# Memory and x read by feature as well: transposes of both left out, k-tiles of memory and weights in turns, memory's scale moved to the split of the values

## The chip, the cores and the metric

The kernel runs on one core of a Trainium2 chip, in one launch. The metric is the device time of one execution in microseconds, the median of several runs. Five engines matter: TensorE (PE; its weight loads are shown apart as PEld), VectorE (DVE), ScalarE (ACT), GpSimd (POOL), and SyncE (SP), which here issues nearly all DMAs. Each engine works through its own queue in order, and waits on semaphores of the others.

## The reference, cut to what matters

One layer of a streaming encoder in float32: 256 tokens, width 2048, 256 memory tokens.

```python
def reference(x, mem, positions, norm_mix_g, w_in, ...):
    h = rms_norm(x, norm_mix_g)
    x = x + hybrid_mixer(h, positions, w_in, conv_w, ...)
    h = rms_norm(x, norm_x_g)
    mem_n = rms_norm(mem, norm_mem_g)
    x = x + cross_attention(h, mem_n, w_xq, w_xkv, w_xo)
    h = rms_norm(x, norm_ffn_g)
    x = x + jnp.square(jax.nn.relu(h @ w_ff1)) @ w_ff2
    return rms_norm(x, norm_final_g)

def rms_norm(x, g):
    y = x * lax.rsqrt(jnp.mean(x * x, axis=-1, keepdims=True) + 1e-6)
    return y * g
...
    k, v = jnp.split(mem_n @ w_kv, 2, axis=-1)      # in cross_attention
```

`rms_norm` has two factors: a gain per feature and a scale per token. A product over the features needs the gain inside, but the token's scale can be multiplied in afterwards, at the rows of the product.

## The kernel before, in words

All large products run as three TensorE products of a cheaper number format (float32r): an operand is split into a rounded part (`whi`, `qh`) and the rest (`wlo`, `ql`), and hi x hi, hi x lo and lo x hi are added up in PSUM. The split of weights is `fetch` (L89): one DMA on SP brings a *quarter* of the features, 4 k-tiles of 128 rows by 512 columns, 1 MiB, into `raw` (3 buffers); ScalarE rounds it in two halves (L108), VectorE subtracts (L111); `whi` and `wlo` have 3 buffers of a half each. SP also issues the loads of all other tensors, in one fixed order.

`chunk` (L137) makes 512 output columns for 256 tokens: for each of the 4 quarters, 4 k-tiles, 2 halves of the tokens and three products (L151, L152, L153) of 512 columns. `blocks` (L177) is the form with weights as the stationary operand (L193, L194).

A *quad* holds 4 k-tiles of activations by feature (feature on the partitions, 256 tokens along the row), hi and lo. Activations come as rows of tokens, so they are transposed on TensorE against `ident`.

The order around the change, at the start of the program:

- `load_gains(0, ...)` (L242): memory's gains arrive as 16 rows and are transposed by TensorE (L248).
- `values(0)` (L334): the first 512 columns of the cross-attention's values. Its `chunk` calls `load_mem(c)` (L325) for each quarter: a load of memory's rows (L312), eight transposes (L262), then on ScalarE rounding with the gain (L275) and on VectorE the rest (L276). The first quarter's weights come in two DMAs (`rush`). The chunk's evacuation multiplies by the token scale of memory (L343), so it first takes the row squares of memory (L291) and `rms_cols`.
- gains of the other norms (L349, 48 rows, one transpose); four loads of x's rows (L352), their squares, `rms_cols`, and `scale_row` (L299), which spreads the scale of the tokens over the partitions as `rrow` by TensorE (L303).
- x by feature: 32 transposes (L364); ScalarE copies them out as `xt` (L367), which SP writes to a scratch `xt_d` in DRAM for the later residual (L368, read in `load_x`, L953); VectorE makes `xn` = x times gain times `rrow` (L371), and a split fills `h1` (L374, L375).
- `values(1)`; the four conv weights come as rows and are transposed by two TensorE instructions (L386); constants, positions, sine and cosine; `values(2)`, `narrow` (L204), `values(3)`; decay tables (L521), and the keys by `blocks` (L545), scaled by `mrow`, memory's scale spread over the partitions.

Then the mixer, the cross-attention (L963 on: keys and values are read back from DRAM and split, L970 and L971) and the MLP follow. The instructions of every engine are put in order ahead of the launch by a scheduler that goes by priorities (`high_priority`) and by its own estimate of when operands are there.

Of the kernel before, what the change touches and what calls it, by code (L numbers as in the profile page):

```python
# [17 lines left out]
P = 128  # L18
# [29 lines left out]
MAGIC = 1.5 * 2.0**23  # L48


@with_exitstack
def trunk(ctx: ExitStack, tc: tile.TileContext, x, mem, positions, norm_mix_g, w_in, conv_w, gdn_a_log, gdn_dt_bias,
          ret_gn_g, gdn_norm_g, w_out, norm_x_g, norm_mem_g, w_xq, w_xkv, w_xo, norm_ffn_g, w_ff1, w_ff2,
          norm_final_g, inv_freq, out):
# [21 lines left out]
    rushed = []  # L76

# [11 lines left out]
    def fetch(pieces, k, n, rush=False, hold=None, at=(0, 0)):  # L89


        raw = wp.tile([P, k * n], F32, name="raw", tag="raw", bufs=3)
        rv = raw.rearrange("p (k n) -> p k n", k=k)
        with tc.high_priority(offset=100000):
            for off, ap in pieces:
                src = ap.rearrange("(k p) n -> p k n", p=P)
                for ks in ((slice(0, k // 2), slice(k // 2, k)) if rush else (slice(0, k),)):
                    fetched.append(nc.sync.dma_start(rv[:, ks, off:off + ap.shape[1]], src[:, ks, :]).ins)
            got = []
            for i in range(2):  # L100
                if hold:
                    both = hold().both
                    hi, lo = (both[:, a:a + 2, :].rearrange("p a s -> p (a s)") for a in (0, 2))
                else:
                    hi, lo = (wp.tile([P, k * n // 2 + room], F32R, name=nm, tag=nm, bufs=3)[:, a:a + k * n // 2]
                              for nm, a, room in zip(("whi", "wlo"), at, (64, 0)))
                src = raw[:, i * k * n // 2:(i + 1) * k * n // 2]
                rounding = act.activation(hi, src, AF.Copy)  # L108
                if rush and not i:
                    rushed.append(rounding.ins)  # L110
                vec.tensor_sub(lo, src, hi.bitcast(F32))  # L111
                got.append((hi.rearrange("p (k n) -> p k n", n=n), lo.rearrange("p (k n) -> p k n", n=n)))
        return got
# [23 lines left out]
    def chunk(quads, pieces_of, evac, before=None, hold=None):  # L137

# [87 lines left out]
    vec.memset(warm, 0.0)  # L226
    act.activation(warm, warm, AF.Exp)
    ident = cp.tile([P, P], F32, name="ident")
    ones = cp.tile([P, P], F32, name="ones")
    vec.memset(ones, 1.0)  # L230
# [9 lines left out]
    gains = cp.tile([P, 64], F32, name="gains")  # L240

    def load_gains(c0, vectors):  # L242
        rows = sm.tile([48, P], F32, name="grow", tag="junk", bufs=1)
        n = 16 * len(vectors)
        for i, g in enumerate(vectors):
            nc.sync.dma_start(rows[16 * i:16 * (i + 1), :], g.rearrange("o (k p) -> (o k) p", p=P))
        gps = bank()
        pe.transpose(gps[:, :n], rows[:n], ident[:n, :n])  # L248
        vec.tensor_copy(gains[:, c0:c0 + n], gps[:, :n])

    with tc.high_priority(offset=200000):
        load_gains(0, (norm_mem_g,))
    G_MEM, G_MIX, G_X, G_FFN = 0, 16, 32, 48

    def to_feature(src, gain, quad):

        for f2 in range(2):
# [8 lines left out]
            qh, ql = quad  # L266
            if gain is None:
                h, l = qh[:, f2 * 2:f2 * 2 + 2, :], ql[:, f2 * 2:f2 * 2 + 2, :]
                act.activation(h, pv, AF.Copy)
                vec.tensor_sub(l, pv, h.bitcast(F32))  # L270
            else:
                for f in range(2):
                    k = f2 * 2 + f
                    g = gains[:, gain + k:gain + k + 1]
                    last = act.activation(qh[:, k, :], pv[:, f, :], AF.Copy, scale=g)  # L275
                    vec.scalar_tensor_tensor(ql[:, k, :], pv[:, f, :], g, qh[:, k, :].bitcast(F32),  # L276
                                             op0=ALU.mult, op1=ALU.subtract)
        return None if gain is None else last.ins
# [28 lines left out]
    def load_rows(c, src, rush, pieces=1):  # L307
        xc = kv.tile([P, NT, 512], F32, name="xc", tag="xc", bufs=8)
        rows = src[0, :, c * 512:(c + 1) * 512].rearrange("(t p) d -> p t d", p=P)
        with tc.high_priority(offset=rush):  # L310
            for ts in (slice(i * NT // pieces, (i + 1) * NT // pieces) for i in range(pieces)):
                nc.sync.dma_start(xc[:, ts, :], rows[:, ts, :])  # L312
# [12 lines left out]
    def load_mem(c):  # L325
        with tc.high_priority(offset=50000):
            xc = load_rows(c, mem, 50000 if c else 100000, 1 if c else 2)
            with tc.high_priority(offset=100000), nullcontext() if c else tc.issue_after(rushed[0]):
                ins = to_feature(lambda t, f: xc[:, t, f * P:(f + 1) * P], G_MEM + 4 * c, memq[c])
        mem_rows.append((xc, ins))  # L330

    mem_scale, mem_rows = [], []

    def values(n):  # L334
        vo = kv.tile([P, NT, 512], F32, name="vo", tag="vo", bufs=2)

        def evac_kv(t, ps, c0, c1):
            if not mem_scale:
                for c in range(4):
                    with tc.issue_after(mem_rows[c][1]):  # L340
                        row_squares(mem_rows[c][0], ssqm, c)
                mem_scale.append(rms_cols("nm", ssqm))
# [6 lines left out]
    load_gains(16, (norm_mix_g, norm_x_g, norm_ffn_g))  # L349
    h1 = [quad_a() for _ in range(4)]  # L350
    ssq1 = cp.tile([P, NT, 4], F32, name="ssq1")
    xcs = [load_rows(c, x, 0) for c in range(4)]  # L352
    for c in range(4):
        row_squares(xcs[c], ssq1, c)
    rstd1 = rms_cols("n1", ssq1)
    rrow = scale_row("rrow", rstd1)
    xt_d = dram.tile([P, KT, S], F32, name="xt_d", tag="xt_d", bufs=1)
    for k2 in range(8):
        ps = bank()
        pv = ps.rearrange("p (f s) -> p f s", f=2)  # L360
        for f in range(2):
            for t in range(NT):
                col = (2 * k2 + f) % 4 * P
                pe.transpose(pv[:, f, t * P:(t + 1) * P], xcs[k2 // 2][:, t, col:col + P], ident)  # L364
        xt = kv.tile([P, 2, S], F32, name="xt", tag="xt", bufs=2)
        xn = kv.tile([P, 2, S], F32, name="xn", tag="xn", bufs=2)
        act.activation(xt, pv, AF.Copy)  # L367
        nc.sync.dma_start(xt_d[:, 2 * k2:2 * k2 + 2, :], xt)  # L368
        for f in range(2):
            k = 2 * k2 + f  # L370
            vec.scalar_tensor_tensor(xn[:, f, :], pv[:, f, :], gains[:, G_MIX + k:G_MIX + k + 1], rrow,  # L371
                                     op0=ALU.mult, op1=ALU.mult)
        qh, ql = (a[:, k2 % 2 * 2:k2 % 2 * 2 + 2, :] for a in h1[k2 // 2])
        act.activation(qh, xn, AF.Copy)  # L374
        vec.tensor_sub(ql, xn, qh.bitcast(F32))  # L375

    values(1)

    cw_rows = kv.tile([96, 2, P], F32, name="cw_rows", bufs=1)
    for a in range(2):  # L380
        for j in range(2):
            nc.sync.dma_start(cw_rows[48 * j:48 * (j + 1), a, :], conv_w[0, 2 * a + j].rearrange("(b p) -> b p", p=P))
    cw = mc.tile([P, 4, 48], F32, name="cw")
    for a in range(2):
        ps = bank()
        pe.transpose(ps[:, :96], cw_rows[:, a, :], ident[:96, :96])  # L386
        vec.tensor_copy(cw[:, 2 * a:2 * a + 2, :], ps[:, :96].rearrange("p (j b) -> p j b", j=2))
# [142 lines left out]
    values(2)  # L530
    narrow(h1, w_in[0], C_GA, 32, decay_rows)
# [4 lines left out]
    rstdm = mem_scale[0]  # L536
# [303 lines left out]
    def gates():  # L840
# [23 lines left out]
        def of_delta_rule(j, yr, yg, quad, before=None):  # L864
            chunk(h1, cols(w_in[0], C_GZ + 512 * j), silu_gate(yg))
            chunk(h1, cols(w_in[0], C_TB + 512 * j), sig_gate(yg, yr), before=before)
            to_feature(lambda t, f: yg[:, t, f * P:(f + 1) * P], None, quad)
# [96 lines left out]
    for h in range(XH):  # L964
# [6 lines left out]
        split(vv, vr)  # L971
# [60 lines left out]
    for fb in range(4):  # L1032
# [67 lines left out]
_INS = ["x", "mem", "positions", "norm_mix_g", "w_in", "conv_w", "gdn_a_log", "gdn_dt_bias", "ret_gn_g", "gdn_norm_g",  # L1100
        "w_out", "norm_x_g", "norm_mem_g", "w_xq", "w_xkv", "w_xo", "norm_ffn_g", "w_ff1", "w_ff2", "norm_final_g"]
# [23 lines left out]
```

## Time and profile before

| | |
|---|---|
| median of 3 runs | 2081.36 us (2081.08 to 2081.57) |
| profiled execution, span of its instructions | 2078.0 us |
| TensorE busy | 2060.9 us (99%) |
| VectorE, ScalarE busy | 1404.6 us, 1115.2 us |
| DMA | 407.21 MB, mean 196 GB/s |

The profile shows one execution. A line of the timeline is: start, length, engine, line of the kernel, operation, output and inputs by the program's names, how many in a row; in brackets the idle time of the engine ahead of it and what ended it. A group's line gives its count, busy time and mean duration, and after the bar the idle time ahead of it. Products are pipelined, so that the next one starts before one has ended: their rate is read from starts. SP's rows show the issue of a DMA, not its transfer.

### The profile page before, as it was taken

The numbers are of one execution on the slowest core, as the hardware profiler recorded it, in microseconds if no ns is written. First come the engines' busy times: TensorE is split into PE (matmuls) and PEld (weight loads), VectorE is DVE, ScalarE is ACT, GpSimd is POOL, SyncE is SP. The second block draws the span as 40 slices with busy tenths as digits, with TensorE's granted clock in tenths as the row PEclk, the third lists the DMA queues.
The fourth block names the chain that finished last, engine by engine and source line by source line (L and its number), as shares of the span: only waits on it lengthen the run. The fifth ranks groups of instructions, "written<-read, shape, count | busy, mean of one in ns | idle before, by whom it ended". The sixth has DMA issues, their size and how long they took to land.

```text
span 2078.0 us, 28543 instructions
## 1 busy us (share of the span) xinstructions
PE 2060.9 (99%) x10996; PEld 1776.8 (86%) x10996; DVE 1404.6 (68%) x2230; ACT 1115.2 (54%) x1835; POOL 30.9 (1%) x37
## 2 busy tenths in 40 slices
PE   8999999999999999999999999999999999999998
PEld 6788888888888888888888899888888888888887
DVE  5766779778757885778557665776556556645655
ACT  7584664675547554655446554654444434434444
POOL 0000000000000000000000000000000000000000
PEclk9999999999999999999999999999999999999999
DMA  8787655556555655555467664579566656556653
GB/s 300 237 274 249 197 188 195 169 177 195 187 163 190 192 181 163 190 187 191 146 213 244 190 190 153 183 204 242 185 200 185 199 185 196 188 199 186 195 190 142
DMA packets 331064, 407.21 MB, mean 196 GB/s; under 512 B 35232, under 2 KB 239024, under 8 KB 330800
## 3 DMA queue, kind: packets, MB, share of 16 engines
q1 hardware_dynamic: 330640, 404.87, 61.1%
q8 instruction: 86, 1.41, 0.3%
q10 hardware_dynamic: 288, 0.52, 0.1%
q14 instruction: 50, 0.41, 0.1%
HBM read 389.61 MB, written 13.65 MB: 194 GB/s over the span
## 4 chain that ended last, share of the span: by engine, by line
PE 95%; DMA 2%; ACT 1%; SPq 1%; DVE 1%; issue 0%; POOLq 0%; POOL 0%; ACTq 0%; DVEq 0%
PE s L193 33%; PE s L194 17%; PE s L152 13%; PE s L153 13%; PE s L151 13%; PE b L709 1%; PE b L616 1%; DMA xc<-x 1%; ACT whi L108 1%; PE b L742 1%; PE b L122 0%; PE b L121 0%; DVE wlo L111 0%; PE b L123 0%; DMA xt_d<-xt 0%; SPq L312 0%
## 5 line engine op out<-in xcount | busy, mean ns | idle before, releaser
L111 DVE TENSOR_TENSOR wlo<-raw,whi 128x1024 fp32r<-128x1024 f32 x700 | 855.5, 1223 | 510.2 <-ACT whi L108 503.8
L108 ACT ACTIVATE whi<-raw 128x1024 fp32r<-128x1024 f32 x700 | 740.6, 1059 | 688.0 <-PE s L153 338.9
L193 PE MATMUL s<-q,whi 128*128 128x512 f32 x3072 | 1056.6, 390 | 0.3 <-DVE q L1006 0.3
L194 PE MATMUL s<-q,wlo 128*128 128x256 f32 x3072 | 839.6, 281 | 0.7 <-DVE wlo L111 0.7
L193 PEld LDWEIGHTS s<-q,whi 128*128 128x128 f32 x3072 | 567.5, 188 | 109.9 <-DVE q L1006 0.5
L194 PEld LDWEIGHTS s<-q,wlo 128*128 128x128 f32 x3072 | 576.2, 188 | 14.4 <-DVE wlo L111 2.6
L152 PE MATMUL s<-wlo,q 128*128 128x512 f32 x1264 | 495.8, 392 | 0.7 <-DVE wlo L111 0.7
L153 PE MATMUL s<-whi,q 128*128 128x512 f32 x1264 | 492.1, 390 | 0.0
L151 PE MATMUL s<-whi,q 128*128 128x512 f32 x1264 | 451.2, 390 | 2.6 <-ACT q L275 2.6
L151 PEld LDWEIGHTS s<-whi,q 128*128 128x128 f32 x1264 | 237.2, 188 | 51.8 <-ACT q L275 3.0
L152 PEld LDWEIGHTS s<-wlo,q 128*128 128x128 f32 x1264 | 237.6, 188 | 49.3 <-DVE wlo L111 2.1
L153 PEld LDWEIGHTS s<-whi,q 128*128 128x128 f32 x1264 | 237.8, 188 | 47.5
L200 ACT ACTIVATE bo<-s 128x256 f32<-128x256 f32 x192 | 72.9, 379 | 121.1 <-PE s L194 107.9
L201 DVE TENSOR_TENSOR bo<-bo,s 128x256 f32<-128x256 f32 x192 | 79.9, 416 | 44.0 <-ACT bo L200 43.7
L569 DVE SCALAR_TENSOR_TENSOR acc<-bo,cw,acc 128x255 f32<-128x255 f32 (+1 forms) x144 | 66.8, 479 | 3.1 <-ACT acc L566 1.2
L678 DVE TENSOR_TENSOR pr<-lw,tw 32x31 f32<-32x31 f32 (+15 forms) x124 | 40.5, 326 | 11.1 <-DMA lw<-scr_l 9.1
L680 DVE TENSOR_TENSOR tw<-tw,pr 32x31 f32<-32x31 f32 (+15 forms) x124 | 40.6, 327 | 2.0
L843 ACT ACTIVATE gth<-s 128x512 f32<-128x512 f32 x32 | 19.0, 594 | 21.6 <-PE s L153 15.1
L1053 DVE SCALAR_TENSOR_TENSOR res<-s,rstd3q,res 128x512 f32<-128x512 f32 (+1 forms) x32 | 22.3, 735 | 12.0 <-PE s L153 12.0
L1040 DVE SCALAR_TENSOR_TENSOR hs<-bo 128x256 f32<-128x256 f32 x64 | 26.9, 421 | 1.1
L1043 DVE TENSOR_TENSOR q<-hs,q 128x256 fp32r<-128x256 f32 x64 | 26.6, 417 | 0.0
L1042 ACT ACTIVATE q<-hs 128x256 fp32r<-128x256 f32 x64 | 26.1, 409 | 0.4 <-DVE hs L1040 0.4
(304 smaller groups left out, 1075.6 us busy)
## 6 DMA issues: line engine op xcount, KB each, us to landing
raw<-w_in SPq DMA_DIRECT2D x143, 1024.0 KB
raw<-w_ff SPq DMA_DIRECT2D x128, 1024.0 KB
raw<-w_xkv SPq DMA_DIRECT2D x31, 1024.0 KB
raw<-w_out SPq DMA_DIRECT2D x16, 1024.0 KB
raw<-w_xq SPq DMA_DIRECT2D x16, 1024.0 KB
raw<-w_xo SPq DMA_DIRECT2D x16, 1024.0 KB
dec_d<-dec_w SPq DMA_DIRECT2D x8, 384.0 KB
dec<-dec_d SPq DMA_DIRECT2D x8, 384.0 KB
```

What stands on the lines that cost most here:

```text
L108: rounding = act.activation(hi, src, AF.Copy)
L111: vec.tensor_sub(lo, src, hi.bitcast(F32))
L151: pe.matmul(o, xh, wh, start=first, stop=False)
L152: pe.matmul(o, xh, wl, start=False, stop=False)
L153: pe.matmul(o, xl, wh, start=False, stop=last)
L193: pe.matmul(ps[b], lh, xhl, start=kk == 0, stop=False)
L194: pe.matmul(ps[b][:, :S], ll, xh, start=False, stop=kk == KT - 1)
L200: act.activation(o, ps[b][:, S:], AF.Copy)
L201: vec.tensor_add(o, o, ps[b][:, :S])
L569: vec.scalar_tensor_tensor(acc[:, d:], ps[:, :S - d], cw[:, j, blk:blk + 1], acc[:, d:], op0=ALU.mult, op1=ALU.add)
L678: vec.tensor_mul(pv, lw[:, j, j + 1:32].unsqueeze(2).to_broadcast([32, n, j + 1]), tw[:, j, 0:j + 1].unsqueeze(1).to_broadcast([32, n, j + ...
L680: vec.tensor_sub(tw[:, j + 1:32, 0:j + 1], tw[:, j + 1:32, 0:j + 1], pv)
```

## The change

The host passes four more arrays: `x_f` and `mem_f` are x and memory by feature ([128, 16, 256]: feature within the k-tile, k-tile, token), `gains_f` the four gain vectors by feature, `conv_f` the conv weights by feature. x and memory are still passed as rows too, for the row squares.

- Gains: one load of 128x64 on ScalarE's DMA queue. Conv weights: one load. No transposes of either.
- Memory: `memory(c)` loads `mem_f` by feature and splits it with the gain straight from SBUF. In the first quarter, memory and weights come in four turns of one k-tile each (`cuts=4`), and are split by k-tile.
- x: `x_f` is loaded by feature for `h1`; `xt`, `xt_d` and the 32 transposes go. `load_x` reads `x_f`.
- The value chunks are evacuated without scale. Memory's rows are loaded a second time, after `values(2)`, for their squares; the scale is applied in the cross-attention, when values are split, token half by token half.
- Eight small products on `ones` stand at the start of TensorE's queue.

```diff
-    def fetch(pieces, k, n, rush=False, hold=None, at=(0, 0)):
+    def fetch(pieces, k, n, cuts=1, along=None, hold=None, at=(0, 0)):
...
-                for ks in ((slice(0, k // 2), slice(k // 2, k)) if rush else (slice(0, k),)):
+                for c in range(cuts):
+                    ks = slice(c * k // cuts, (c + 1) * k // cuts)
+                    if along:
+                        along[0](ks)
                     fetched.append(nc.sync.dma_start(rv[:, ks, off:off + ap.shape[1]], src[:, ks, :]).ins)
...
-                rounding = act.activation(hi, src, AF.Copy)
-                if rush and not i:
-                    rushed.append(rounding.ins)
-                vec.tensor_sub(lo, src, hi.bitcast(F32))
+                part = k * n // max(cuts, 2)
+                for c in range(0, k * n // 2, part):
+                    cs = slice(c, c + part)
+                    act.activation(hi[:, cs], src[:, cs], AF.Copy)
+                    if along:
+                        along[1](slice(i * k // 2 + c // n, i * k // 2 + (c + part) // n))
+                    vec.tensor_sub(lo[:, cs], src[:, cs], hi[:, cs].bitcast(F32))
...
-                halves = fetch(pieces_of(q), 4, 512, rush=before is not None and q == 0)
+                halves = fetch(pieces_of(q), 4, 512, cuts=1 if q else cuts, along=along(q) if along else None)
...
+    with tc.high_priority(offset=300000):
+        vec.memset(ones, 1.0)
+        vec.memset(warm, 0.0)
+        act.dma_start(gains, gains_f)
+        act.activation(warm, warm, AF.Exp)
+        early = bank()
+        for _ in range(WARM):
+            pe.matmul(early[:, :P], ones, ones, start=True, stop=True)
...
+    def memory(c):
+        xf = kv.tile([P, 4, S], F32, name="xc", tag="xc", bufs=8)
+
+        def load(ks):
+            nc.sync.dma_start(xf[:, ks], mem_f[:, 4 * c + ks.start:4 * c + ks.stop])
+
+        def rounded(ks):
+            qh, ql = memq[c]
+            for k in range(ks.start, ks.stop):
+                g = gains[:, G_MEM + 4 * c + k:G_MEM + 4 * c + k + 1]
+                act.activation(qh[:, k, :], xf[:, k], AF.Copy, scale=g)
+                vec.scalar_tensor_tensor(ql[:, k, :], xf[:, k], g, qh[:, k, :].bitcast(F32),
+                                         op0=ALU.mult, op1=ALU.subtract)
+
+        return load, rounded
...
-            act.activation(vo[:, t, :], ps, AF.Copy, scale=mem_scale[0][:, t:t + 1])
+            act.activation(vo[:, t, :], ps, AF.Copy)
...
-        chunk(memq, cols(w_xkv[0], D + n * 512), evac_kv, before=load_mem if n == 0 else None)
+        chunk(memq, cols(w_xkv[0], D + n * 512), evac_kv, cuts=1 if n else 4, along=None if n else memory)
...
+    def norm_of(name, src, ssq):
+        for c in range(4):
+            row_squares(load_rows(c, src), ssq, c)
+        return rms_cols(name, ssq)
+
     values(0)
...
+    rstd1 = norm_of("n1", x, ssq1)
+    values(1)
+    rrow = scale_row("rrow", rstd1)
     for c in range(4):
...
+        xf = kv.tile([P, 4, S], F32, name="xc", tag="xc", bufs=8)
+        nc.sync.dma_start(xf, x_f[:, 4 * c:4 * c + 4])
+        for k2 in range(2):
+            xn = kv.tile([P, 2, S], F32, name="xn", tag="xn", bufs=2)
+            for f in range(2):
+                k = 2 * k2 + f
+                vec.scalar_tensor_tensor(xn[:, f, :], xf[:, k, :], gains[:, G_MIX + 4 * c + k:G_MIX + 4 * c + k + 1],
+                                         rrow, op0=ALU.mult, op1=ALU.mult)
+            split([a[:, 2 * k2:2 * k2 + 2, :] for a in h1[c]], xn)
...
+    nc.sync.dma_start(cw, conv_f)
...
     values(2)
+    rstdm = norm_of("nm", mem, ssqm)
     narrow(h1, w_in[0], C_GA, 32, decay_rows)
     values(3)
...
-        nc.sync.dma_start(xc, xt_d[:, 2 * b2:2 * b2 + 2, :])
+        nc.sync.dma_start(xc, x_f[:, 2 * b2:2 * b2 + 2, :])
...
-        split(vv, vr)
+        for t in range(NT):
+            r = rstdm[:, t:t + 1]
+            act.activation(vv[0][:, t], vr[:, t], AF.Copy, scale=r)
+            vec.scalar_tensor_tensor(vv[1][:, t], vr[:, t], r, vv[0][:, t].bitcast(F32), op0=ALU.mult, op1=ALU.subtract)
```

More of the change, by code (lines that the diff above doesn't have):

```diff
@@ L1 @@
 import math
-from contextlib import ExitStack, nullcontext
+from contextlib import ExitStack
 import numpy as np
@@ L48, with trunk @@
 MAGIC = 1.5 * 2.0**23
+WARM = 8
 @with_exitstack
-def trunk(ctx: ExitStack, tc: tile.TileContext, x, mem, positions, norm_mix_g, w_in, conv_w, gdn_a_log, gdn_dt_bias,
-          ret_gn_g, gdn_norm_g, w_out, norm_x_g, norm_mem_g, w_xq, w_xkv, w_xo, norm_ffn_g, w_ff1, w_ff2,
-          norm_final_g, inv_freq, out):
+def trunk(ctx: ExitStack, tc: tile.TileContext, x, mem, x_f, mem_f, positions, gains_f, w_in, conv_f, gdn_a_log,
+          gdn_dt_bias, ret_gn_g, gdn_norm_g, w_out, w_xq, w_xkv, w_xo, w_ff1, w_ff2, norm_final_g, inv_freq, out):
     nc = tc.nc
@@ L135, in quad_a, with chunk @@
         return new_quad(hqp, 5)
-    def chunk(quads, pieces_of, evac, before=None, hold=None):
+    def chunk(quads, pieces_of, evac, before=None, hold=None, cuts=1, along=None):
         ps = stream_ps()
@@ L238, in rsqrt, with to_feature @@
         pool.tensor_tensor(o, i, nhalf_pow[:, :o.shape[1]], op=ALU.pow)
[L240 to L252, printed above, removed]
     G_MEM, G_MIX, G_X, G_FFN = 0, 16, 32, 48
-    def to_feature(src, gain, quad):
+    def to_feature(src, quad):
         for f2 in range(2):
@@ L265, in to_feature @@
                 continue
[L266 to L278, printed above, removed]
+            split([a[:, f2 * 2:f2 * 2 + 2, :] for a in quad], pv)
     def rms_cols(name, ssq, count=D):
@@ L305, in scale_row, with load_rows @@
         return row
-    def load_rows(c, src, rush, pieces=1):
+    def load_rows(c, src):
         xc = kv.tile([P, NT, 512], F32, name="xc", tag="xc", bufs=8)
[L309 to L312, printed above, removed]
+        nc.sync.dma_start(xc, src[0, :, c * 512:(c + 1) * 512].rearrange("(t p) d -> p t d", p=P))
         return xc
@@ L353, in trunk @@
+    values(1)
+    rrow = scale_row("rrow", rstd1)
     for c in range(4):
[L354 to L375, printed above, removed]
@@ L383, in trunk @@
     cw = mc.tile([P, 4, 48], F32, name="cw")
[L384 to L387, printed above, removed]
+    nc.sync.dma_start(cw, conv_f)
     trimask = kv.tile([P, P], F32, name="trimask", bufs=1)
@@ L535, in trunk @@
         decays(h2)
-    rstdm = mem_scale[0]
     mrow = scale_row("mrow", rstdm)
@@ L1097, in trunk, with _by_feature @@
                   hold=quad_b if last else None)
-_INS = ["x", "mem", "positions", "norm_mix_g", "w_in", "conv_w", "gdn_a_log", "gdn_dt_bias", "ret_gn_g", "gdn_norm_g",
-        "w_out", "norm_x_g", "norm_mem_g", "w_xq", "w_xkv", "w_xo", "norm_ffn_g", "w_ff1", "w_ff2", "norm_final_g"]
+_INS = ["x", "mem", "positions", "w_in", "gdn_a_log", "gdn_dt_bias", "ret_gn_g", "gdn_norm_g", "w_out", "w_xq", "w_xkv",
+        "w_xo", "w_ff1", "w_ff2", "norm_final_g"]
+def _by_feature(rows):
+    return np.ascontiguousarray(rows.T.reshape(-1, P, rows.shape[0]).transpose(1, 0, 2))
 def _inv_freq():
@@ L1117 @@
     arrays["inv_freq"] = _inv_freq()
+    arrays["x_f"] = _by_feature(inputs["x"][0])
+    arrays["mem_f"] = _by_feature(inputs["mem"][0])
+    arrays["gains_f"] = np.concatenate([_by_feature(inputs[n])[:, :, 0] for n in
+                                        ("norm_mem_g", "norm_mix_g", "norm_x_g", "norm_ffn_g")], axis=1)
+    arrays["conv_f"] = _by_feature(inputs["conv_w"][0]).transpose(0, 2, 1).copy()
     for name, a in arrays.items():
```

28 lines of the change are left out of this document (3 added, 25 removed).

## The prediction

> **What bounds the kernel now.** First the page: its busy line and the chain of waits.
>
> ```profile
> span 2078.0 us, 28543 instructions
> PE 2060.9 (99%) x10996; PEld 1776.8 (86%) x10996; DVE 1404.6 (68%) x2230; ACT 1115.2 (54%) x1835; POOL 30.9 (1%) x37
> PE 95%; DMA 2%; ACT 1%; SPq 1%; DVE 1%; issue 0%; POOLq 0%; POOL 0%; ACTq 0%; DVEq 0%
> ```
>
> TensorE sets the end nearly everywhere. Whatever takes a place in its queue is paid in full, and whatever other engines do is free until a product waits for it. The change touches the first 130 us and a little of the cross-attention, so I next read TensorE's timeline there.
>
> ```profile
> 4.45 0.69 PE L262 MATMUL b<-ident,xc 128*128 128x128 f32 x2 [1.74 <-DMA xc<-mem]
> 5.75 1.54 PE L262 MATMUL b<-ident,xc 128*128 128x128 f32 x6 [0.62 <-DMA xc<-mem]
> 9.94 1.22 PE L151 MATMUL s<-whi,q 128*128 128x512 f32 x2 [2.65 <-ACT q L275]
> ...
> 18.27 0.62 PE L151 MATMUL s<-whi,q 128*128 128x512 f32 x2
> 18.73 1.03 PE L262 MATMUL b<-ident,xc 128*128 128x128 f32 x8
> 19.52 0.48 PE L152 MATMUL s<-wlo,q 128*128 128x512 f32 x1
> 19.84 0.39 PE L153 MATMUL s<-whi,q 128*128 128x512 f32 x1
> ...
> 36.28 0.39 PE L153 MATMUL s<-whi,q 128*128 128x512 f32 x1
> ```
>
> The columns are start, length and the instruction; in brackets stands idle time. Two overlapping products last 0.62 us and one 0.39 us, so 512-column products follow each other 0.23 us apart. The first product comes at 9.94 us, 5.5 us after the first transpose, and the first two last 1.22 us, so they are 0.6 us apart. The eight transposes at 18.73 delay the next product to 19.52 (0.79 us), and that one holds the next for 0.32 us rather than 0.23: 0.88 us for eight. The first chunk has 96 products (4 quarters, 4 k-tiles, 2 token halves, 3 products), 21.8 us at 0.227; its products end, and those of the second chunk begin, at about 36.3 us.
>
> Is a transfer or a rounding behind this? The queue of SP, the chain of waits in order of time, ScalarE's timeline and the windows say so:
>
> ```profile
> 0.79 0.40 SPq L246 DMA_DIRECT2D grow<-norm_mem_g  x1
> 1.24 0.89 SPq L312 DMA_DIRECT2D xc<-mem  x2
> ...
> 9.26 5.09 SPq L312 DMA_DIRECT2D xc<-x  x4
> ...
> 22.05 0.38 SPq L98 DMA_DIRECT2D raw<-w_xkv  x1
> ```
> ```profile
> 13.04 11.95 DMA xc<-x
> ...
> 28.80 5.47 DMA raw<-w_xkv
> ...
> 34.35 1.07 ACT whi L108
> ```
> ```profile
> 8.47 1.06 ACT L108 ACTIVATE whi<-raw 128x1024 fp32r<-128x1024 f32 x1 [5.39 <-DMA raw<-w_xkv]
> 28.51 2.01 ACT L108 ACTIVATE whi<-raw 128x1024 fp32r<-128x1024 f32 x2 [0.17 <-DMA raw<-w_xkv]
> ```
> ```profile
> 10.00:20.00 10.00, 10.00 (x44) 8.25 (x45) 7.77 (x13) 9.55 (x21) 0.00 (x0) 1.00 1.04 390
> 26.00:31.00 5.00, 5.00 (x24) 4.14 (x23) 3.60 (x11) 4.73 (x11) 0.78 (x1) 1.00 0.65 175
> ```
>
> The last column of the windows is GB/s. From 10 to 20 us the transfers run at 390 GB/s, so 1 MiB of weights takes 2.7 us and half a MiB of x or memory 1.35 us. The last x tile lands at 13.04 + 11.95 = 25.0 us; by then 7 MiB have come (three quarters of weights, memory, x). The fourth quarter of weights, issued behind all of x, is rounded from 28.5 us. The fifth lands at 34.27 and its rounding starts at 34.35, 2 us before its products are due at 36.3. So in the first 36 us the transfers are nearly as late as TensorE; a start that is 5 us earlier can be used only as far as weights three and four quarters on come earlier too.
>
> **The change, part by part.**
>
> *The start.* The gains' load leaves SP (0.45 us, from the issues at 0.79 and 1.24), the transposes of memory's first quarter go, and a quarter of mem_f and of weights comes as four k-tiles of 128 + 256 KB in turns. Before, 256 KB let the first transpose start at 4.45, 512 KB the next at 5.75. A first pair of 384 KB lies between, 5.1, less 0.45: 4.65 us. A rounding of 128x512 costs 0.63:
>
> ```profile
> L213 ACT ACTIVATE whi<-raw 128x512 fp32r<-128x512 f32 x1 | 0.6, 632 | 0.5 <-ACT whi L108 0.5
> L291 ACT ACTIVATE junk<-xc 128x512 f32<-128x512 f32 x16 | 10.0, 624 | 0.2
> L367 ACT ACTIVATE xt<-b 128x512 f32<-128x512 f32 x8 | 4.5, 596 | 3.9 <-DMA xt_d<-xt 3.9
> ```
>
> So the first product is at 5.3 us instead of 9.94. The second quarter, however, is one transfer of 1 MiB behind 2 MiB of others. Before, 1 MiB had landed at 8.47; two more at 390 GB/s take 5.4 us, so 13.4 us after the shift, and with one rounding (1.06) its products start at 14.5. The first quarter's 24 products (5.4 us; twice that at the slow pace of the start) fit in between with waits. From 14.5 the other 72 products need 16.3 us: at best the chunk ends at 30.9, 5.4 us earlier than now. That is one end.
>
> The other end is the order on SP. If the fourth quarter still stands behind all four x loads, it lands at 25.0 - 0.45 + 2.7 = 27.2 and is multiplied from 28.3; TensorE wanted it at 14.5 + 2 x 5.4 = 25.4 and waits 2.9 us. The chunk then ends at 33.7, a gain of 2.6. The fifth quarter came 5.8 us behind the fourth (28.5 to 34.27), with small loads in between and the transfers half idle (175 GB/s). The same distance gives 33.0, products from 34.1: the gain falls to 2.2. One tile of x_f in front of it (they become free to load when a tile of mem_f is used up) adds 1.35: 0.9. With no small loads between, 2.6 stays. Worst, all of x_f goes ahead (5.4) and nothing is gained: 0. I choose **2.4**, since the order of before (x first) is the nearest row, and since three of conv_w's four small loads and the gains' loads leave the queue.
>
> *Memory's other transposes* (three groups) are in these times already. *x's transposes* go from TensorE:
>
> ```profile
> 56.55 0.61 PE L303 MATMUL b<-ident,n_r 128*128 128x128 f32 x4
> 57.00 1.47 PE L364 MATMUL b<-ident,xc 128*128 128x128 f32 x12
> 58.23 0.47 PE L151 MATMUL s<-whi,q 128*128 128x512 f32 x1
> ...
> 62.20 0.60 PE L364 MATMUL b<-ident,xc 128*128 128x128 f32 x4
> 62.56 0.48 PE L153 MATMUL s<-whi,q 128*128 128x512 f32 x1
> ```
>
> Twelve take 57.00 to 58.23, 1.23 us; four take 0.36 and 0.09 of slower restart, 0.45, and there are three such groups; the remaining eight cost 0.88 as above. Together 1.23 + 3 x 0.45 + 0.88 = **3.5 us**, in a stretch where products follow each other without idle time.
>
> *The gains' second transpose and the two of conv_w:*
>
> ```profile
> 39.77 0.26 PE L248 MATMUL b<-ident,grow 48*128 48x48 f32 x1
> 39.96 0.50 PE L152 MATMUL s<-wlo,q 128*128 128x512 f32 x1
> 40.30 0.39 PE L153 MATMUL s<-whi,q 128*128 128x512 f32 x1
> ...
> 71.10 0.25 PE L386 MATMUL b<-ident,cw_rows 96*128 96x96 f32 x1
> 71.12 0.48 PE L152 MATMUL s<-wlo,q 128*128 128x512 f32 x1
> ```
>
> 39.77 to 39.96 and 0.11 of restart, with some 0.09 before it: 0.4 us. A transpose of conv_w takes 0.02 before its successor, and 0.1 of restart: 0.25 for both. **0.6 us.**
>
> *Bubbles that the removed work made:*
>
> ```profile
> 51.44 0.50 PE L152 MATMUL s<-wlo,q 128*128 128x512 f32 x1 [0.29 <-DVE wlo L111]
> ...
> 75.55 0.50 PE L152 MATMUL s<-wlo,q 128*128 128x512 f32 x1 [0.39 <-DVE wlo L111]
> ```
>
> At 51.44 ScalarE is full of row squares; at 75.55 the queue behind eight evacuations xt has been held by transfers (the row L367: 3.9 us waiting for xt_d). The evacuations go (4.5 us of ScalarE), and memory's squares move from before 36 us to after the third value chunk. With the 0.1 of restart they cost about 1 us; bounds 0 (others take their place) and 1.2. I take **1.0**.
>
> *What is added.* Eight warming products: L303 stands for two calls with four records, 57.00 - 56.55 = 0.45 us, so 0.22 a call, 1.8 us for eight, or 3.6 at the slow pace; they begin after a memset near 1 us and end before the first product at 5.3. Hidden by the first transfers; uncovered at most 3.6 us of start, which the wait for the second quarter would swallow. The memory rows are loaded a second time, 4 x 1.35 = 5.4 us of transfers; xt_d's 2 MiB of writes go, x_f's 2 MiB of reads come. The squares' count is the same (16 x 0.62 us). They lie beside products in a stretch where weights use half of the bandwidth (1 MiB for 5.4 us of products); cost nothing as long as ScalarE doesn't stand in a square whose row is late. The h1 build reads SBUF rather than PSUM with the same instruction: nothing.
>
> *Values split with the scale:*
>
> ```profile
> L117 ACT ACTIVATE vvh<-vr 128x1024 fp32r<-128x1024 f32 x4 | 4.2, 1060 | 2.2 <-PE b L122 1.8 <-DMA vr<-vv_d 0.4
> L118 DVE TENSOR_TENSOR vvl<-vr,vvh 128x1024 fp32r<-128x1024 f32 x4 | 4.9, 1226 | 3.1 <-ACT vvh L117 3.1
> ```
>
> One of 1.06 becomes two of 0.63 on ScalarE, +0.2; on VectorE one of 1.23 becomes two, between two halves of 0.62 (+0) and, with a start of its own for each, +0.5. Per head 0.2 to 0.7 us, hidden by the q-projection's products of the same head; uncovered 0.8 to 2.8 us for four heads. I take 0.
>
> The sum: 2.4 + 3.5 + 0.6 + 1.0 = 7.5 us off the profiled span: 2078.0 - 7.5 = 2070.5. The runs' median is 2081.36, 3.4 us above the span; I keep that: **2073.9 us**.
>
> By the Trainium skill (TensorE: Matmul & The Clock Gate, Part 1) the array runs at half clock until it has been busy for a window of about 3.4 us, and falls back after an idle one. The trace agrees on the first half: six transposes last 1.54 us at 5.75, eight 1.03 at 18.73. By it the warming products speed up the first quarter, but the idle 3 us before the second could take the clock back, an estimate of up to 1.7 us; the full-gain rival below would then be 2072.6, the forecast unchanged, since there the fourth quarter's arrival decides.
>
> **The rivals.**
>
> *Full gain at the start*: the fourth and fifth quarters go ahead of x and x_f. For it: they carry the highest priority, and x isn't needed until 57 us. Against it: before, x stood first. 5.4 + 3.5 + 0.6 + 1.0 = 10.5: 2070.9.
>
> *The start is eaten by the transfers*: x and x_f stand ahead of the fifth quarter. For it: the fifth quarter is already only 2 us early. Against: 26 to 31 us has room (175 of 390 GB/s, about 1 MB). Start 0, the rest 5.1 or, with new waits in the second chunk of about 1.5, 3.6: 2076.3 to 2077.8.
>
> *Slower: ScalarE stands in row squares.* In its fixed order, squares that wait for the rows of memory (four loads, 5.4 us, behind weights) and cost 8 x 0.81 = 6.5 us themselves (0.62 and the 0.19 that 3.0 us over 16 accumulator reads come to) stand ahead of roundings of the fourth value chunk.
>
> ```profile
> L291 ACT ACTIVATION_READ_ACCUMULATOR junk<-xc 128x1 f32 x16 | 3.0, 188 | 0.0
> ```
>
> TensorE has a lead of two halves of a quarter, 2 x 2.7 us, less rounding and subtraction (1.06 + 1.23): 3.1 us. From there each microsecond shows: up to 5.4 + 6.5 - 3.1 = 8.8, so 2073.9 + 8.8 = 2082.7; if x's rows do the same in the first two chunks, 2091.5. For it: at 51.44 squares did delay a product. Against: by 0.5 us only, with eight of them in the way.
>
> **How the numbers follow.** About 0.2% (4.2 us) is what a measurement here tells from no change: faster means below 2077.2, slower above 2085.5. Chances: forecast 0.57 (its own range 2071.5 to 2076.2), full gain 0.15, start eaten 0.14 (half below 2077.2), ScalarE's squares 0.14 (0.09 beyond 2085.5). Faster 0.57 + 0.15 + 0.07 = 0.79; same 0.07 + 0.05 = 0.12; slower 0.09. The range runs from a full gain with 1 us more at the start, 2069.9, to a start that is eaten with one more microsecond of waits, 2079.
>
> **What would show it.** Right: a first 512-column product near 5.3 us; the second quarter's rounding near 13.4; the chunk's end near 34; no transposes on TensorE from 10 to 75 us, and 4.1 us of products moved up for them; idle time at 51 and 75 gone. Wrong: x_f or x issued ahead of the fifth quarter with TensorE idle near 31 to 37 us; whi roundings that start late behind squares between 60 and 115 us; TensorE idle in the cross-attention ahead of products on vvl; or a later stage in which products are no longer 0.23 us apart, which nothing here foresees.

## The result and the profile after

The changed kernel took 2087.08 us (2085.09 to 2087.64, 8 runs) against 2081.11 (2080.26 to 2082.06, 8 runs) of the kernel before: ratio 1.0029, interval [1.0018, 1.0039]. It is slower by 0.3%, where 0.36% faster was forecast. The profiled execution's span is 2085.9 us, 7.9 more than before.

First TensorE's timeline of the changed kernel, in which L153, L154 and L155 are the three products of a chunk (L151 to L153 before):

```profile
1.10 3.78 PE L238 MATMUL b<-ones 128*128 128x128 f32 x16 [1.10 <-DVE warm L233]
5.08 0.95 PE L153 MATMUL s<-whi,q 128*128 128x512 f32 x2 [0.20 <-ACT whi L111]
...
14.40 0.74 PE L153 MATMUL s<-whi,q 128*128 128x512 f32 x2 [2.56 <-ACT whi L111]
15.65 0.66 PE L154 MATMUL s<-wlo,q 128*128 128x512 f32 x1 [0.52 <-DVE wlo L114]
16.11 0.63 PE L155 MATMUL s<-whi,q 128*128 128x512 f32 x1
16.54 0.63 PE L154 MATMUL s<-wlo,q 128*128 128x512 f32 x1
...
33.03 0.39 PE L155 MATMUL s<-whi,q 128*128 128x512 f32 x1
...
37.74 1.22 PE L153 MATMUL s<-whi,q 128*128 128x512 f32 x2 [3.89 <-ACT whi L111]
...
53.38 0.73 PE L153 MATMUL s<-whi,q 128*128 128x512 f32 x2 [0.85 <-ACT whi L111]
55.46 0.50 PE L154 MATMUL s<-wlo,q 128*128 128x512 f32 x1 [1.35 <-DVE wlo L114]
62.91 0.73 PE L153 MATMUL s<-whi,q 128*128 128x512 f32 x2 [2.13 <-ACT whi L111]
64.17 0.79 PE L154 MATMUL s<-wlo,q 128*128 128x512 f32 x1 [0.53 <-DVE wlo L114]
...
70.42 0.39 PE L155 MATMUL s<-whi,q 128*128 128x512 f32 x1
...
118.35 0.63 PE L195 MATMUL s<-q,whi 128*128 128x512 f32 x2
```

The kernel before had its last product of the second chunk, and its first product of the keys, here:

```profile
60.84 0.39 PE L153 MATMUL s<-whi,q 128*128 128x512 f32 x1
...
112.04 0.63 PE L193 MATMUL s<-q,whi 128*128 128x512 f32 x2
```

Up to 33 us the forecast times hold: first product at 5.08 us, second quarter at 14.40, last product of the first chunk at 33.03 instead of 36.28, a gain of 3.25. Then TensorE waits 3.9 us for the second chunk's first weights, and again inside this chunk; its last product comes at 70.42 instead of 60.84, a loss of 9.6. So the second chunk lost 12.8 us, although twelve of the 32 transposes and a bubble left it. The other 20 transposes and the bubble in the third chunk are gone too, and by the keys 3.3 us are back (118.35 against 112.04, 6.3 late). Two longer waits near 135 us add 0.9, and 0.7 is spread over the rest.

The windows of the same trace show a second loss. A row gives the stretch and its length, the busy time of PE, PEld, DVE, ACT and POOL, then the granted clock of TensorE (1.00 is full speed, 0.50 half), the DMA share and GB/s.

```profile
10.00:20.00 10.00, 6.92 (x23) 4.90 (x22) 7.46 (x14) 7.79 (x15) 0.00 (x0) 0.83 1.04 393
20.00:30.00 10.00, 10.00 (x46) 8.28 (x45) 5.26 (x9) 8.88 (x20) 0.29 (x1) 1.00 0.95 347
30.00:40.00 10.00, 6.08 (x24) 4.42 (x23) 7.48 (x19) 5.95 (x11) 0.41 (x1) 0.82 0.81 279
40.00:50.00 10.00, 9.47 (x35) 7.26 (x34) 9.50 (x18) 7.23 (x16) 0.00 (x0) 0.84 1.02 375
...
60.00:70.00 10.00, 7.34 (x26) 5.30 (x25) 4.30 (x4) 6.58 (x9) 0.00 (x0) 0.83 0.59 194
```

A mean of 0.83 over 10 us is 3.4 us at half clock and the rest at full; together 13.6 us in three stretches, each just behind a wait. There products last 0.63 us and follow each other 0.43 us apart (16.11 to 16.54) instead of 0.23. In the kernel before the same windows show 1.00.

Why the weights are late stands in SP's queue of the changed kernel:

```profile
10.32 1.34 SPq L98 DMA_DIRECT2D raw<-w_xkv  x1
11.71 4.91 SPq L292 DMA_DIRECT2D xc<-x  x2
16.66 1.19 SPq L343 DMA_DIRECT2D xc<-x_f  x1
17.89 0.60 SPq L353 DMA_DIRECT2D cw<-conv_f  x1
18.61 0.55 SPq L343 DMA_DIRECT2D xc<-x_f  x1
...
21.29 3.18 SPq L365 DMA_DIRECT2D invf<-inv_freq  x2
...
31.16 0.40 SPq L98 DMA_DIRECT2D raw<-w_xkv  x1
...
32.21 1.23 SPq L343 DMA_DIRECT2D xc<-x_f  x2
33.53 0.58 SPq L292 DMA_DIRECT2D xc<-mem  x1
34.20 0.47 SPq L98 DMA_DIRECT2D raw<-w_xkv  x1
34.76 1.40 SPq L292 DMA_DIRECT2D xc<-mem  x2
```

The fourth weights are issued at 10.32 us, the second chunk's first weights only at 31.16 us (28.80 before). Between them stand two tiles of x, two tiles of x_f and eight small transfers (seven loads and the write of a decay table, `dm_d`). SP issued several of the small ones only when an older, larger transfer had landed; two of its waits (in total, times, longest, in us):

```profile
SPq L412 <- DMA xc<-x_f: 2.6, 1, 2.6
SPq L365 <- DMA raw<-w_xkv: 2.1, 1, 2.1
```

The second chunk's other weights are mixed with the rest of x_f and with memory's rows, which the program has only behind the third chunk. That fits the buffers: all these tiles share eight, those of x's rows come free with the last square of x, which begins at 28.5 us, and memory's rows are issued from 33.53 us on.

### The profile page after: what moved, and what is told of

It reads as the page before. It is cut to its first block, busy times and chain, and to the rows that moved or that the text cites. A ratio compares the mean times of both kernels' runs of the same rounds, so it can differ in the third digit from the quotient of the medians.

```text
span 2085.9 us, 28421 instructions
## 1 busy us (share of the span) xinstructions
PE 2062.5 (99%) x10944; PEld 1774.3 (85%) x10944; DVE 1405.2 (67%) x2232; ACT 1115.8 (53%) x1835; POOL 30.7 (1%) x37
## 4 chain that ended last, share of the span: by engine, by line
PE 95%; DMA 2%; ACT 1%; issue 0%; SPq 0%; DVE 0%; POOLq 0%; POOL 0%; ACTq 0%
PE s L195 33%; PE s L196 17%; PE s L154 13%; PE s L155 13%; PE s L153 13%; DMA raw<-w_xkv 1%; PE b L675 1%; DMA xc<-x_f 1%; PE b L582 1%; PE b L708 1%; PE b L125 0%; PE b L124 0%; PE b L126 0%; ACT whi L111 0%; ACT dec_w L487 0%
## 5 line engine op out<-in xcount | busy, mean ns | idle before, releaser
L114 DVE TENSOR_TENSOR wlo<-raw,whi 128x1024 fp32r<-128x1024 f32 (+1 forms) x702 | 855.2, 1219 | 516.4 <-ACT whi L111 509.7
L111 ACT ACTIVATE whi<-raw 128x1024 fp32r<-128x1024 f32 (+1 forms) x702 | 740.7, 1057 | 691.2 <-PE s L155 350.1
L154 PE MATMUL s<-wlo,q 128*128 128x512 f32 x1264 | 497.9, 394 | 3.0 <-DVE wlo L114 2.9
L155 PE MATMUL s<-whi,q 128*128 128x512 f32 x1264 | 494.0, 391 | 0.0
L153 PE MATMUL s<-whi,q 128*128 128x512 f32 x1264 | 451.6, 391 | 9.6 <-ACT whi L111 9.6
L153 PEld LDWEIGHTS s<-whi,q 128*128 128x128 f32 x1264 | 237.7, 189 | 61.0 <-ACT whi L111 12.1
L154 PEld LDWEIGHTS s<-wlo,q 128*128 128x128 f32 x1264 | 238.8, 189 | 54.5 <-DVE wlo L114 6.8
L155 PEld LDWEIGHTS s<-whi,q 128*128 128x128 f32 x1264 | 238.8, 189 | 47.9
```

What stands on the lines that cost most here:

```text
L111: act.activation(hi[:, cs], src[:, cs], AF.Copy)
L114: vec.tensor_sub(lo[:, cs], src[:, cs], hi[:, cs].bitcast(F32))
L153: pe.matmul(o, xh, wh, start=first, stop=False)
L154: pe.matmul(o, xh, wl, start=False, stop=False)
L155: pe.matmul(o, xl, wh, start=False, stop=last)
```

## The experiments

Each run is compared with runs of the kernel before on the same chip (medians 2080.5 to 2080.8 us).

**Memory's rows moved, and only their squares moved.** `late_mem` queues the four row loads of memory on SP behind the third chunk's last weights:

```diff
         for c in range(4):
-            row_squares(load_rows(c, src), ssq, c)
+            with tc.issue_after(fetched[-1]) if name == "nm" else nullcontext():
+                xc = load_rows(c, src)
+            row_squares(xc, ssq, c)
```

> The changed kernel with one thing moved: the four loads of memory's rows are issued on SP behind the last weight load of the third value chunk, instead of ahead of the second chunk's weights. Theory (the order on SP: x_f, small loads and memory's rows stand ahead of the second chunk's weights, and each wait also drops TensorE's clock to half): the wait of 4.2 us before the second chunk and its slow clock stay; the waits inside the second chunk (0.7, 1.2, 1.5, 2.5 us and a slow window, together about 7 us) mostly go: 2079 to 2082 us. Rival (ScalarE stands in squares, h1 roundings and table loads): memory's squares move with their rows, so it expects a gain of this size too; the run sq_late tells them apart. Rival (the added work itself, such as the scaled split of values, costs the time): no gain, 2087.

`sq_late` leaves the loads and queues the squares on ScalarE behind the roundings of the third chunk (`roundings` holds the rounding instructions of `fetch`):

```diff
+            xc = load_rows(c, src)
+            with tc.issue_after(roundings[-1]) if name == "nm" else nullcontext():
+                row_squares(xc, ssq, c)
```

> The changed kernel with memory's row loads where they are, but the eight row squares of memory queued on ScalarE behind the roundings of the third value chunk. Theory (order on SP): the weights of the second chunk come as late as before, so little is gained: 2084 to 2087 us. Rival (ScalarE stands in squares): the 6.5 us of squares leave the second chunk, and 4 to 7 us are gained: 2080 to 2083.

Measured: `late_mem` 2079.79 us, ratio to before 0.9996 [0.9987, 1.0005]; `sq_late` 2083.49, 1.0012 [1.0002, 1.0021]. TensorE's waits between 30 and 72 us in `late_mem`:

```profile
37.19 1.22 PE L153 MATMUL s<-whi,q 128*128 128x512 f32 x2 [3.04 <-ACT whi L111]
38.91 0.79 PE L154 MATMUL s<-wlo,q 128*128 128x512 f32 x1 [0.50 <-DVE wlo L114]
```

and in `sq_late`:

```profile
39.13 0.73 PE L153 MATMUL s<-whi,q 128*128 128x512 f32 x2 [3.04 <-ACT whi L111]
40.85 0.80 PE L154 MATMUL s<-wlo,q 128*128 128x512 f32 x1 [0.99 <-DVE wlo L114]
55.45 0.50 PE L154 MATMUL s<-wlo,q 128*128 128x512 f32 x1 [0.67 <-DVE wlo L114]
61.04 0.73 PE L153 MATMUL s<-whi,q 128*128 128x512 f32 x2 [0.31 <-ACT whi L111]
62.30 0.50 PE L154 MATMUL s<-wlo,q 128*128 128x512 f32 x1 [0.52 <-DVE wlo L114]
```

Without memory's rows the waits inside the second chunk are gone but for 0.50 us behind its first two products, and 7.3 us are gained by the medians; the wait before it stays. With the squares alone moved, the waits inside shrink from 5.4 us (the four rows from 53 to 64 us in the changed kernel, and one of 0.53 at 47 us) to 2.5, and half of the gain, 3.6 us, appears. The profiled execution of `sq_late` is its slowest, 2086.64 us, with a first chunk that ends at 35.26 us instead of 33.03 though the edit doesn't touch it; so compare the second chunk by itself, from its first product to its last: 32.7 us in the changed kernel, 28.1 in `sq_late`, 25.0 in `late_mem`, 24.3 before. Neither theory was right alone: the rows delay the weights in the queue (in the changed kernel those issued at 34.20 us landed 10.63 us later), and their squares delay the roundings on ScalarE. A row of ScalarE's timeline of the changed kernel shows how that looks:

```profile
59.67 0.42 ACT L394 ACTIVATE cos<-ang 128x256 f32<-128x256 f32 x1
60.11 1.28 ACT L492 ACT_TABLE_LOAD   x1
61.41 0.51 ACT L492 ACTIVATE dm_w<-dist,lnk 128x256 f32<-128x256 f32 x1
61.82 1.99 ACT L111 ACTIVATE whi<-raw 128x1024 fp32r<-128x1024 f32 x2
```

The rounding for which TensorE waits from 60.6 to 62.9 us stands behind cosine, a table load and a decay table.

**The queue mended.** `late_all` also puts x_f behind the second chunk's weights and the small loads behind its first weights; `late_both` leaves the small loads as they are:

```diff
+        with tc.issue_after(fetched[-1]):
+            nc.sync.dma_start(xf, x_f[:, 4 * c:4 * c + 4])
...
+    with tc.issue_after(fetched[7]):
+        nc.sync.dma_start(cw, conv_f)
```

(the second edit likewise for positions, inverse frequencies, `gdng`, `alog`, `dtb` and `dm_d`; only in `late_all`).

> The changed kernel with SP's order mended at three places: x_f behind the weights of the second value chunk, memory's rows behind those of the third, and the small loads (conv_f, positions, inverse frequencies, decays and the like) behind the first weights of the second chunk. Theory (order on SP): TensorE doesn't wait for the second chunk, the clock stays up after 20 us, and the gain of 3.3 us that the changed kernel has at the end of the first chunk is kept, with 4 to 5 us from the transposes of x: 2072 to 2075 us, faster than the kernel before. Rival (ScalarE): h1 is built later, in 6 us less room, and its roundings collide with weights': 2078 to 2083. Rival (the work itself): 2087.

> As late_all, but the small loads (conv_f, positions and so on) stay ahead of the first weights of the second value chunk; x_f and memory's rows are behind weights. If x_f and memory's rows are what made the second chunk late, this keeps nearly all of late_all's gain: 2074 to 2077 us. If the small loads, each of which takes one of the queue's outstanding places, were the larger part of the wait of 4.2 us, the wait stays near 3 us with its slow window: 2078 to 2081.

Measured: `late_all` 2074.93 us, 0.9970 [0.9957, 0.9983]; `late_both` 2077.72, 0.9984 [0.9974, 0.9993]. TensorE's timeline of `late_all` at the change of chunks and its windows:

```profile
33.56 0.39 PE L155 MATMUL s<-whi,q 128*128 128x512 f32 x1
33.79 0.61 PE L286 MATMUL b<-ident,n_r 128*128 128x128 f32 x4
34.15 0.71 PE L153 MATMUL s<-whi,q 128*128 128x512 f32 x2
```
```profile
20.00:30.00 10.00, 10.00 (x46) 8.25 (x45) 5.61 (x9) 9.52 (x22) 0.00 (x0) 1.00 0.97 349
30.00:40.00 10.00, 9.87 (x46) 7.89 (x44) 4.98 (x12) 5.20 (x10) 0.70 (x1) 1.00 0.75 249
```

The second chunk follows the first without a wait, and the clock stays up after 20 us. The same work in another order of loads takes 12.2 us less than the changed kernel and beats the kernel before. The small loads account for some 2.8 of them by the medians, so that `late_both` falls between its two expectations; in it the wait before the second chunk is 2.2 us:

```profile
35.69 0.73 PE L153 MATMUL s<-whi,q 128*128 128x512 f32 x2 [2.22 <-ACT whi L111]
```

**The clock.** `fill` puts twelve products whose result isn't used into the wait before the second quarter of the changed kernel; `warm0` takes the eight warming products out of it.

```diff
+            if along and q == 1:
+                with tc.issue_after(ended[-1]), tc.high_priority(offset=200000):
+                    for _ in range(12):
+                        pe.matmul(early[:, :P], ones, ones, start=True, stop=True)
```

> The changed kernel with twelve small products on ones queued on TensorE between the first and the second quarter of the first chunk, where it waits 2.95 us; their result isn't used. Theory (idle time drops the clock for a window of 3.4 us): the products from 15.6 to 19.4 us come 0.23 us apart instead of 0.43, and the first chunk ends 1.8 us earlier; since the second chunk's weights are late whatever TensorE does, the wait before it grows by as much and the total stays within 1 us of 2087. Rival (the slow products have another cause, such as transfers that contend for memory): they stay 0.43 us apart.

> The changed kernel without the eight warming products. Theory: the first quarter's products come at 0.43 us apart and end near 12.5 instead of 11.7 us; the second quarter's weights land at the same time and the end of the first chunk moves by at most 2 us, all of it hidden by the wait for the second chunk: within 1 us of 2087, so that the warming is worth nothing here. Rival (the early clock matters): 2 to 4 us slower, 2089 to 2091.

Measured: `fill` 2085.73 us, 1.0022 [1.0013, 1.0031]; `warm0` 2086.00, 1.0022 [1.0013, 1.0032]. In `fill` the timeline reads

```profile
12.21 2.84 PE L161 MATMUL b<-ones 128*128 128x128 f32 x24
14.80 0.71 PE L153 MATMUL s<-whi,q 128*128 128x512 f32 x2
...
16.10 0.40 PE L155 MATMUL s<-whi,q 128*128 128x512 f32 x1
16.34 0.39 PE L154 MATMUL s<-wlo,q 128*128 128x512 f32 x1
...
37.36 1.22 PE L153 MATMUL s<-whi,q 128*128 128x512 f32 x2 [4.22 <-ACT whi L111]
```

(A product of two float32 operands has two records, so x24 are the twelve.) The same products now follow each other 0.24 us apart instead of 0.43: the wait made them slow, not the transfers beside them, which run at 394 GB/s here and at 393 in the changed kernel. The first chunk ends 0.7 us earlier (its last product starts at 32.31 us) rather than the 1.8 expected, and part of that goes to the longer wait behind it (4.22 instead of 3.89). The total is 1.4 us lower by the medians, where at most 1 was expected.

`warm0` is no slower than the changed kernel. Its first products are 0.43 us apart up to 10.5 us, so the first quarter ends later, the wait before the second is 0.85 us instead of 2.56, and no slow products follow it. The first chunk's last product starts at 31.26 us, 1.8 earlier than with the warming products; the wait for the second chunk (4.68 us) takes this up. So here the warming products only moved the slow products from the first quarter to the second.

A wait doesn't always bring the half clock. Both `warm0` and `fill` wait 2.68 and then 0.53 us, with two products between, near 60 us; the windows that follow, `warm0` first, then `fill`:

```profile
60.00:70.00 10.00, 9.24 (x32) 7.18 (x33) 5.21 (x5) 7.47 (x10) 0.00 (x0) 0.83 0.70 217
60.00:70.00 10.00, 9.02 (x38) 7.17 (x39) 5.95 (x5) 7.93 (x11) 0.00 (x0) 1.00 0.82 257
```

What decides between the two, no run here shows.

**x alone.** `x_only` is the kernel before with x's part only: `h1` from x_f, loaded behind the second chunk's weights; transposes, `xt` and `xt_d` gone.

```diff
-                pe.transpose(pv[:, f, t * P:(t + 1) * P], xcs[k2 // 2][:, t, col:col + P], ident)
...
+        with tc.issue_after(fetched[-1]):
+            nc.sync.dma_start(xf, x_f[:, 4 * c:4 * c + 4])
```

> The kernel before with x's part of the change alone: h1 is built from x_f, loaded behind the second value chunk's weights; the 32 transposes, xt and xt_d go; memory's start, gains and scale stay as before. The prediction's terms are 3.5 us for the transposes and up to 1 for bubbles: 2076.5 to 2078 us. Rival (the transposes' places in the queue are refilled with waits): no difference from before, 2081.

Measured: 2076.72 us, 0.9979 [0.9970, 0.9989]: 4.1 us less by the medians. From 50 to 77 us its timeline shows no wait of TensorE at all; the two bubbles of before are gone.

**Further with the start.** `late_q1` is `late_all` with the second quarter in turns of k-tiles too, `late_q12` with the second and the third, and with the small loads and x's rows behind the second chunk's first weights (its edit has no hold for x's rows; they come there by the scheduler's order); `late_all_fill` is `late_all` with the filling products.

```diff
-halves = fetch(pieces_of(q), 4, 512, cuts=1 if q else cuts, along=along(q) if along else None)
+halves = fetch(pieces_of(q), 4, 512, cuts=cuts if q < 2 or not along else 1, along=along(q) if along else None)
```

(`late_q1`; `late_q12` has `q < 3`. With more loads ahead, `fetched[7]` in `late_q1` is the second quarter's last k-tile instead of the second chunk's first weights, so that conv_f is issued ahead of those weights there.)

> late_all, and the second quarter of the first chunk also comes in turns of k-tiles of memory and weights. Theory (the second quarter waits for its one transfer of 1 MiB, then runs at half clock): the wait of 2.9 us shrinks to under 1, the clock stays up, the first chunk ends 2 to 4 us earlier, and 1 to 3 us of it are kept: 2072 to 2074 us. Rival (the fourth quarter's weights and the second chunk are late whatever the start does): 2075, as late_all.

> late_all, with the first three quarters of the first chunk coming in turns of k-tiles, and x's rows and the small loads behind the second chunk's first weights. Theory (the wait of 2.9 us goes to the first transfer that is taken as a whole: the second quarter in late_all, the third in late_q1): no wait of over 1 us in the first chunk, no slow window, its end near 30 us; 2071 to 2073.5 us. Rival (weights can't come faster than the transfers' 390 GB/s and the waits move on to the fourth quarter or the second chunk): 2074 to 2075.

> late_all with the twelve filling products between the first and the second quarter (as in fill; their result isn't used). Theory: in late_all the clock is at half from 16.1 to 19.5 us only because of the wait before; filled, it stays up, some 1.8 us of slow products go, and since no later wait takes them up again, part of it arrives at the end: 2073 to 2074 us against 2074.9. Rival (the fourth quarter's or the second chunk's weights set the pace there): 2075, the waits after the second quarter grow by 1.5 us.

Measured: `late_q1` 2074.82 us, 0.9966 [0.9953, 0.9979]; `late_q12` 2074.38, 0.9969 [0.9957, 0.9981]; `late_all_fill` 2073.35, 0.9963 [0.9950, 0.9977]. None differs from `late_all` beyond the intervals, so for `late_q1` and `late_q12` the rivals hold and not the theories. In `late_q1` the wait only moves to the next transfer that is taken whole, and the slow products with it (21.92 lasts 0.63):

```profile
20.16 0.73 PE L153 MATMUL s<-whi,q 128*128 128x512 f32 x2 [2.86 <-ACT whi L111]
...
21.92 0.63 PE L155 MATMUL s<-whi,q 128*128 128x512 f32 x1
```

With the filling products the clock is 1.00 from 10 to 60 us in `late_all_fill`. That is the fastest version tried by its median, at a ratio of 0.9963 to the kernel before.

## Why the prediction was wrong, point by point

- *The start* came out at the forecast times: first product 5.08 (5.3 forecast), second quarter 14.40 (14.5), first chunk 3.25 us earlier (2.6 forecast if the fourth quarter stands behind x). The first two came about as the prediction says; the third is partly luck. The prediction put the fourth weights behind all four loads of x and had TensorE wait 2.9 us for them. In the changed kernel they were issued ahead of the last two, and TensorE didn't wait for them. The chunk lost 2.5 us all the same against the 16.3 us that its last 72 products need, to a wait of 0.5 us and to the products at half clock behind 14.40. `fill` and `warm0` show that TensorE's own pace there hardly mattered to the total, since the wait for the second chunk took it up.
- *The fifth quarter* (the second chunk's first weights) is the first step that failed. The prediction kept its distance from the fourth, 5.8 us, and allowed for one or, at worst, all tiles of x_f ahead, with "nothing is gained" as the bound. That bound doesn't follow from its own sum: 2.2 us less the 5.4 for all of x_f is a loss of 3.2. Measured: ScalarE rounds the fourth weights from 24.07 us and the fifth from 36.64, 12.6 us apart; TensorE waits 3.9 us, and the second chunk begins 1.2 us later than before. The rival that the transfers eat the start named this order, and its sign, x_f ahead of the fifth quarter with TensorE idle near 31 to 37 us, is what the trace shows; it priced all new waits in the second chunk at 1.5 us. `late_all` undoes the loss.
- *Memory's rows* are the second, and larger, failed step. The prediction placed their loads and squares where the program has them, "beside products in a stretch where weights use half of the bandwidth", at no cost. They were issued 30 us earlier than `late_mem` issues them, among the second chunk's weights, and cost some 7 us. The rival of ScalarE's squares had a price range (up to 8.8 us) that holds this, but the wrong place, the fourth value chunk; `sq_late` gives the squares 3.6.
- *The clock.* The prediction saw that an idle stretch of 3 us might take it back, priced this once, at 1.7 us, in the rival only, and left the forecast unchanged because the fourth quarter's arrival would decide; it didn't. Half clock came behind three waits, and each of these cost more than its length. Behind 62.9 us, for example, the products from 64.17 to 67.20 us take 3.0 us where seven at 0.23 us take 1.6, so that 1.4 us come on top of waits of 2.7.
- *x's transposes, small transposes, bubbles* (3.5, 0.6, 1.0 us): right for x, 4.1 us in `x_only` against 3.5 to 4.5. The gains' and conv_w's transposes were not tried alone.
- *The scaled split of values* takes 718 ns twice in place of 1060 on ScalarE and 750 ns twice in place of 1226 on VectorE, per head 0.38 and 0.27 us more, together within the 0.2 to 0.7 that was forecast. It wasn't undone by itself, but the traces bound it: from the first load of `w_out` (1058.56 us before, 1066.08 after) to the first of `w_ff` (1350.15 and 1357.91), a stretch that holds all value splits, the changed kernel falls back by 0.2 us, and `x_only`, which has the old split, by 0.4. So nothing of the loss is seen there, as forecast.

Most of the sum of 7.5 us comes about once the loads are in order. In `late_all` the second chunk begins at 34.15 us against 36.51, the 2.4 us that the prediction chose, the keys begin at 106.20 against 112.04, and the whole is 5.9 us faster than before. With the filled wait it is 7.2, but the filling products are no part of the change that was forecast.

## What to carry to other kernels

A load that is moved or added has two places: where the program has it and where the scheduler issues it. If its buffer is free it may go tens of microseconds early, ahead of the transfers that the bounding engine needs next; so ask, for every added load, what its earliest possible place is, and pin it behind the weights where that hurts. And a wait on TensorE can cost more than its length, since in several of these runs, though not in all, the products behind it ran at half clock.

## What the runs showed of the hardware

SP's queue did not run far ahead here. In the kernel before, the fourth weights were the 20th load by SP's timeline and were issued at 22.05 us; behind them small loads were issued one by one as much earlier and larger ones landed, which suggests that a load of 0.2 KB takes as much of the queue's lead as one of 1 MiB. In the changed kernel the six waits of the small loads from 19.9 to 29.7 us end with landings of x, x, weights, x, x and x_f, the order in which these stand eight places further ahead in the queue. No run here tried it by itself, and whether the chip or the program sets the limit isn't shown. In the changed kernel ten issues take from 17.9 to 31.2 us, while the transfers run at 347 GB/s from 20 to 30.

The half clock came in stretches of 3.4 us or twice that (0.83 of 10 us; 0.82 and 0.84 of two neighbouring ones), in the changed kernel behind waits as short as 2.1 and 0.5 us with two products between them, in `late_q12` behind 1.06 and 0.52 (at 23.82 and 25.08 us). Waits of 2.68 and 0.53 us in `fill` and of 2.22 and 0.53 in `late_both` brought none. For the first 10 us of `warm0` the windows give a clock of 1.00, though its products there are 0.43 us apart: at the start of a trace the spacing of products is the better witness.
